# The second sweep's conv-branch channel gates moved from the merge to between the first sweep's scores

## The chip, the cores and the metric

One core of a Trainium2 chip runs the program. The metric is the device time of one execution in microseconds (us). The kernel before took 1878.28 us (median of 3 runs, 1877.82 to 1882.60).

## What is computed

One decoder layer for a prompt of 512 tokens and 64 sample tokens. A gated short convolution and a sliding-window attention run side by side; per-channel sigmoid gates merge them; a layer norm follows, and then a product-key retrieval over 128 x 128 experts (16 of 128 keys on each side, then 16 of the pairs, for each of 8 heads). Cut to what matters here:

```python
z = x @ w_in                    # b_gate, c_gate, h_in, q, k, v, g_conv, g_attn
conv_y  = short_conv(c_gate * h_in)
conv_br = (b_gate * conv_y) @ w_conv_out
attn_br = attention(q, k, v) @ w_attn_out
merged  = sigmoid(g_conv) * conv_br + sigmoid(g_attn) * attn_br
h = layer_norm(ALPHA * x + merged @ w_o)
top16 of (h @ w_pq) . sub_keys -> 16 experts a head, softmax gate
y = layer_norm(ALPHA * h + sum gate * gelu(h . expert_u[i]) * expert_v[i])
```

## The kernel before, in words

Every matmul is made of three, on values split in a high and a low part: a weight tile of 128 x 1024 is loaded on SP's queue (`raw`), rounded by ACT (`whi`, L119), and the rest is subtracted by POOL or DVE (`wlo`, L120). `table` does this, and `weight` (L580) calls it for the projections and counts the tiles of a sweep in `units`.

The tokens run in two sweeps. The first has 256 columns: prompt chunk 0, the samples and 64 more prompt rows. Its experts are fetched row by row with indirect DMAs on POOL and applied on DVE. The second has 320 columns (chunks 1 to 3) and treats its experts densely, all 128 x 128 of them, as matmuls.

Around the change the program says, in this order: the first sweep's merge, up to its normed `hT`; then the letters of `ORDER` (L62, L829): q and k project the second sweep, each s scores a quarter of the first sweep's keys (`scores`: four products with `w_pq`, matmuls with the keys, then on DVE `top16`, L413 to L417, and after every second s `route`, which gives the expert numbers), each c one of four tiles of the second sweep's convolution, each a one of its three attention chunks. Then the row work of the first sweep is made ready (`experts`, L836), and the second sweep is merged: `merge_conv` (L647) with 8 products for the conv gates (`w_g`, sigmoid on ACT at L658) and 8 with `w_cc` (multiplied on DVE at L661), and `merge_attention` (L663) with the same for the attention branch (L671 to L675), `w_o` and the norm. The tiles of attention and convolution lie in a pool `t`, which `merge_attention` closes before it opens its own, so it starts on the gates only when the last attention is done.

The row work is 384 jobs: a fetch on POOL (L511) and one DVE instruction on 128 x 1024 (L525 for the first 192, L534 for the rest). It is advanced by the generator `side`: a weight tile that is handed a pace calls `side(pace)` behind its own split. In the second sweep tiles up to `PACE_N` have pace (1, 0), but there the row work isn't made yet and nothing runs; later tiles up to 50 have (2, 1, 1) by `units % 3`, and a tile with `units % 4 == 3` is split on DVE and has no pace. `front` (the dense experts' first matmuls) has (2, 1) on its first 69 tiles, and `back` (their last matmuls, 128 steps) has 1 job a step for the first 60 and 3 a step after. What is left at the end is run without pace.

A planner puts each engine's instructions in order ahead of time: of those that its own clock takes for ready it picks the one that stands first in the program. On the chip each engine then keeps that order.

Of the kernel before, what the change touches and what calls it, by code (L numbers as in the profile page):

```python
# [17 lines left out]
AF = mybir.ActivationFunctionType  # L18
ALU = mybir.AluOpType
# [26 lines left out]
DENSE = [1, 2, 3]  # L46
# [12 lines left out]
OB = 3  # L59


ORDER = "qkscscasacsca"  # L62
FQ = 5
KEEP = 10
LAST = 2


PACE_N = 18
PACE_A, PACE_B, PACE_U, PACE_V = (1, 0), (2, 1, 1), (2, 1), (1, 3)
LO_N = 50  # L70
GATED = "aaag"
# [4 lines left out]
def step_kernel(ctx: ExitStack, tc: tile.TileContext, I: dict, O: dict):  # L76
    nc = tc.nc
    V, A, G, PE, S = nc.vector, nc.scalar, nc.gpsimd, nc.tensor, nc.sync

    pools = {}  # L80

    def pool(key, side, bufs=1):
        return tc.tile_pool(name=key, bufs=bufs, side=side)
# [18 lines left out]
    def tmp(p, shape, tag, name=None, bufs=1, dt=F32):  # L102
        return pools[p].tile(shape, dt, tag=tag, name=name or tag, bufs=bufs)
# [163 lines left out]
    def attend_prompt(c, pt, pk, ahi, alo, col):  # L267

        r = pk.shape[1]
        q0 = START[c]  # L270
        k0 = max(0, q0 - 128)
        nk = q0 + r - k0
        use = 64 if c == SMP else 0
        qT = tmp("t", [128, 4, 128], "qT", bufs=2)[:, :, :r]
        A.activation(qT, pt, AF.Copy)
        V.tensor_copy(kT_all[:, q0 + use:q0 + r], pk[:, use:])

        if c == 0:
            blocks = [(0, 128, 0, 0)]
        elif c == SMP:  # L280
            blocks = [(0, 128, 0, 0), (64, 128, 64, 1)]
        else:
            blocks = [(0, 128, 0, c), (128, r, 0, c + 1)]
        mask = mask_p[:r, k0 + 128 - q0:k0 + 128 - q0 + nk]
        o = tmp("t", [128, 4, 2, 64], "o", bufs=2)[:r]
        for kv in range(2):
            st = tmp("t", [128, 1024], "t4", bufs=3)[:r].rearrange("p (g k) -> p g k", g=4)[:, :, :nk]
            for gp2 in range(2):
                ps = bank("at")[:r]
                for j in range(2):  # L290
                    PE.matmul(ps[:, j * 256:j * 256 + nk], qT[kv * 64:kv * 64 + 64, gp2 * 2 + j, :],
                              kT_all[kv * 64:kv * 64 + 64, k0:k0 + nk], start=True, stop=True)
                V.scalar_tensor_tensor(st[:, gp2 * 2:gp2 * 2 + 2, :],
                                       ps.rearrange("p (j k) -> p j k", j=2)[:, :, :nk], SCALE,
                                       mask.unsqueeze(1).broadcast_to([r, 2, nk]), op0=ALU.mult, op1=ALU.add)
            rd = softmax_parts(st, sink_p[:r, kv * 4:kv * 4 + 4], "p")
            pT = tmp("t", [128, 1024], "t4", bufs=3).rearrange("p (b g n) -> p b g n", b=2, g=4)[:, :, :, :r]
            for b, (at, n, _, _) in enumerate(blocks):
                ps = bank("at")
                for g in range(4):  # L300
                    PE.transpose(ps[:n, g * 128:g * 128 + r], st[:, g, at:at + n], ident[:r, :r])
                src = ps[:n].rearrange("p (g n) -> p g n", g=4)[:, :, :r]
                if b == 0:
                    A.activation(pT[:n, b], src, AF.Copy)
                else:
                    V.tensor_copy(pT[:n, b], src)
            po = bank("at")[:r]
            in_order([((po[:, g * 64:(g + 1) * 64], pT[lo:n, b, g, :], v_all[lo:n, vb, kv * 64:kv * 64 + 64]),
                       dict(start=(b == 0), stop=(b == len(blocks) - 1)))
                      for g in range(4) for b, (_, n, lo, vb) in enumerate(blocks)])  # L310
            V.tensor_tensor(o[:, :, kv, :], po[:, :256].rearrange("p (g d) -> p g d", g=4),
                            rd.unsqueeze(2).broadcast_to([r, 4, 64]), op=ALU.mult)
        pa = bank("at")
        for g in range(4):
            PE.transpose(pa[:, g * 128:g * 128 + r], o[:, g].rearrange("p k d -> p (k d)"), ident[:r, :r])
        split(ahi[:, :, col + use:col + r], alo[:, :, col + use:col + r],
              pa.rearrange("p (g n) -> p g n", g=4)[:, :, use:r])

    def attend_sample(pt, pk, v, kc, vc, ahi, alo, col):
# [4 lines left out]
        qf = qT.rearrange("p b g t -> p (b g t)")  # L324
        mask_s = tmp("t", [128, 2, 192], "mask_s")
        late(mask_s, I["mask_s"])
        st = tmp("t", [128, 1024], "t4", bufs=3)[:, :768].rearrange("p (k b s) -> p k b s", k=2, b=2)
        for kv in range(2):
            r = slice(kv * 64, kv * 64 + 64)
            ps = bank("at")  # L330
            for bh in range(2):
                o0 = bh * 192
                PE.matmul(ps[:, o0 + 128:o0 + 192], qf[r, bh * 128:(bh + 1) * 128], kT[r, :], start=True, stop=True)
                for bl in range(4):
                    b = bh * 4 + bl
# [8 lines left out]
        for i in range(4):  # L344
            PE.transpose(pc[:, i * 128:(i + 1) * 128], sf[:, i, :128], ident)
            PE.transpose(pn[:64, i * 128:(i + 1) * 128], sf[:, i, 128:192], ident)
        pcn = tmp("t", [128, 2, 4, 128], "t4", bufs=3)
        pcT, pnT = pcn[:, 0], pcn[:64, 1]
        V.tensor_copy(pcT, pc.rearrange("p (i n) -> p i n", i=4))
        A.activation(pnT, pn[:64].rearrange("p (i n) -> p i n", i=4), AF.Copy)  # L350
# [210 lines left out]
    def lhs(T, k, i):  # L561
        return tuple(t[:, k, i * 128:min(i * 128 + 128, t.shape[2])] for t in T)

    def begin(w, chunks, rows, segs, smp):
        s = SimpleNamespace(w=w, chunks=chunks, n=len(chunks), rows=rows, segs=segs, smp=smp, units=0)
        s.mv = sum(rows)
        s.xs = ExitStack()
        pools["t"] = s.xs.enter_context(pool(f"t{w}", "right"))
        s.xT = pair("x", "x", 8, s.mv)
        s.pieces = iter(list(enumerate(zip(pieces[w], pieces[w][1:]))))  # L570
        load_x(s)
        return s
# [7 lines left out]
    def weight(s, src):  # L580
        s.units += 1
        if s.w == 0:
            return table(src, "w", G if s.units % 3 != 1 else V)
        if s.units > LO_N:
            return table(src, "w", G)
        pace = PACE_A if s.units <= PACE_N else PACE_B
        if s.units % 4 == 3:
            return table(src, "w", V)
        return table(src, "w", G, pace[s.units % len(pace)])

    def product(s, wt, T, ks, tag, k0=0):

        ps = bank(tag)[:, :s.mv]
        for k in range(ks):
            mm3(ps, block(wt, k0 + k), tuple(t[:, k, :s.mv] for t in T), k == 0, k == ks - 1)
        return ps
# [28 lines left out]
    def attention(s, i):  # L625
        c = s.chunks[i]
        q, k, v = s.qkv[i]

        if c in (2, 3):
            for name, t in (("ck_p", k), ("cv_p", v)):  # L630
                S.dma_start(O[name][(c - 2) * 64:(c - 1) * 64], t[(3 - c) * 64:])
        pt, pk = transpose_qk(q, k)
        if c == SMP:
            kc = tmp("g", [128, 8, 128], "g", name="kc", bufs=GBUF)
            late(kc, I["kcT"])
            vc = tmp("g", [128, 8, 128], "g", name="vc", bufs=GBUF)
            late(vc, I["vc"])
            S.dma_start(O["ck_s"][:, 120:128, :], k[:64, :])
            S.dma_start(O["cv_s"][:, 120:128, :], v[:64, :])
            attend_sample(pt, pk, v, kc, vc, *s.at, i * 128)  # L640
        attend_prompt(c, pt, pk, *s.at, i * 128)

    def conv(s, ct):
        conv_tile(ct, lambda j: product(s, weight(s, I["w_bch"][ct, j]), s.xT, 8, "u" if j else "mm"), *s.cv,
                  s.segs, s.smp)

    def merge_conv(s):  # L647

        if s.smp:
            S.dma_start(O["sc_s"], state)  # L650
        if 3 in s.chunks:
            S.dma_start(O["sc_p"], ucar)
        s.rs = ExitStack()
        pools["r"] = s.rs.enter_context(pool(f"r{s.w}", "left"))
        s.br = tmp("r", [128, 8, s.mv], "br")
        for dt in range(8):
            sg = tmp("t", [128, s.mv], ("cg", "bg")[dt % 2])
            A.activation(sg, product(s, weight(s, I["w_g"][dt, 0]), s.xT, 8, "u"), AF.Sigmoid)  # L658
            if dt % 2 == 0:
                wt = weight(s, I["w_cc"][dt // 2])  # L660
            V.tensor_tensor(s.br[:, dt, :], sg, product(s, wt, s.cv, 4, "mm", dt % 2 * 4), op=ALU.mult)  # L661

    def merge_attention(s):  # L663

# [146 lines left out]
    at_stack = ExitStack()  # L811
    pools["at"] = at_stack.enter_context(psum("at", 3))
    sel3 = ([tmp("k", [128, 128], f"k3{k}") for k in range(2)], tmp("k", [128, 128], "gt3"))
    first = begin(0, GATHER, [128, 128], [(0, 128), (192, 256)], 128)
    project_q(first)
    project_kv(first)
# [1 line left out]
        attention(first, i)  # L818
    for ct in range(4):
        conv(first, ct)  # L820
    merge_conv(first)
    merge_attention(first)
    for src, dst in (("ck", "ck_s"), ("cv", "cv_s")):
        late(O[dst][:, 0:120, :], I[src][:, 8:128, :])
    second = begin(1, DENSE, [128, 128, 64], [(0, 320)], 0)
    do = dict(q=lambda: project_q(second), k=lambda: project_kv(second), s=lambda: scores(first, count["s"]),
              c=lambda: conv(second, count["c"]), a=lambda: attention(second, count["a"]))
    count = dict.fromkeys(do, 0)
    for x in ORDER:  # L829
        do[x]()  # L830
# [218 lines left out]
```

## Time and profile before

| | us |
|---|---|
| median of 3 runs | 1878.28 |
| lowest, highest | 1877.82, 1882.60 |
| the profiled execution's own time | 1882.06 |
| its span, first to last instruction | 1880.3 |
| PE busy | 1733.5 |
| DVE busy | 1507.2 |
| POOL busy | 1111.2 |
| ACT busy | 782.1 |

PE is the matmul engine, DVE, ACT and POOL the vector, scalar and general engine; SP only issues DMAs. A row of a timeline gives the start, the duration, the engine, the line, the operation, the tiles (out<-in) and, in brackets, how long the engine had been idle and what released it. A row of a list of groups gives count, busy time, mean, and idle time before.

### The profile page before, as it was taken

Reading aid. Unit: us, or ns where it says so; the run is one execution under the profiler, and the core shown is the slowest. Engines: PE = TensorE matmul, PEld = TensorE weight load, DVE = VectorE, ACT = ScalarE, POOL = GpSimd, SP = SyncE. Lnnn points to the kernel's source line nnn. Section 1 sums busy time; section 2 is a strip of 40 time slices with the busy share of each in tenths; the row PEclk is TensorE's granted clock in tenths of the full one; section 3 lists DMA queues with packets and bytes.
Section 4 is the critical chain, followed back from the end, with each engine's and each line's share of the span. In section 5 each row is a group of like instructions: output and inputs, shape, how many; then the busy total and the mean of one; then the engine's idle time right before and its main releaser. Section 6 shows DMA issues by size and latency. Waiting matters only on the chain.

```text
span 1880.3 us, 27617 instructions
## 1 busy us (share of the span) xinstructions
PE 1733.5 (92%) x9760; PEld 1573.5 (84%) x9760; DVE 1507.2 (80%) x2632; ACT 782.1 (42%) x1339; POOL 1111.2 (59%) x724
## 2 busy tenths in 40 slices
PE   7999998897989998699979899999999999999985
PEld 7997798887779888699978777787899999998974
DVE  6646689998955699998896677878778888888897
ACT  4554343442333433367785333333333333343322
POOL 4445433466756667688835522223578777778883
PEclk9999999997989999799999899999999999999998
DMA  7445443357757678799947999999989999989973
GB/s 246 156 134 213 130 135 118 113 186 254 277 192 249 232 239 276 248 326 363 338 187 253 330 327 328 345 336 341 322 311 353 335 327 353 350 299 339 326 264 108
DMA packets 190539, 496.50 MB, mean 264 GB/s; under 512 B 17712, under 2 KB 83696, under 8 KB 187312
## 3 DMA queue, kind: packets, MB, share of 16 engines
q1 hardware_dynamic: 135104, 293.39, 45.5%
q0 software_dynamic: 55296, 201.35, 30.1%
q8 instruction: 76, 1.25, 0.3%
q14 instruction: 63, 0.52, 0.1%
HBM read 454.48 MB, written 40.54 MB: 263 GB/s over the span
## 4 chain that ended last, share of the span: by engine, by line
PE 49%; DVE 24%; DMA 10%; issue 7%; POOL 5%; ACT 5%; SPq 1%; DVEq 0%; POOLq 0%; ACTq 0%
PE acc L937 19%; PE ps L123 9%; PE ps L124 8%; PE ps L125 8%; POOL wlo L120 3%; DMA re<-spill 3%; DVE junk L525 3%; PE ps L794 2%; POOL g L511 2%; DVE wlo L120 2%; DMA raw<-in_euT 2%; ACT whi L119 1%; ACT hot L791 1%; DMA g<-in_eu,idx 1%; DVE s L415 1%
## 5 line engine op out<-in xcount | busy, mean ns | idle before, releaser
L120 POOL TENSOR_TENSOR wlo<-raw,whi 128x1024 fp32r<-128x1024 f32 x232 | 580.0, 2503 | 320.6 <-ACT whi L119 287.9
L119 ACT ACTIVATE whi<-raw 128x1024 fp32r<-128x1024 f32 x388 | 409.2, 1056 | 590.0 <-PE ps L124 235.9
L123 PE MATMUL ps<-xhi,whi 128*128 128x384 f32 (+2 forms) x1600 | 531.3, 332 | 34.3 <-ACT sp L860 27.8
L125 PE MATMUL ps<-xhi,wlo 128*128 128x384 f32 (+2 forms) x1600 | 527.4, 330 | 1.6 <-POOL wlo L120 1.6
L124 PE MATMUL ps<-xlo,whi 128*128 128x384 f32 (+2 forms) x1600 | 527.6, 330 | 0.0
L534 DVE SCALAR_TENSOR_TENSOR h<-g,pre,h 128x1024 f32<-128x1024 f32 x192 | 316.2, 1647 | 71.7 <-DMA g<-in_ev,idx 70.4
L511 POOL DMA_INDIRECT g<-in_eu,idx x192 | 206.6, 1076 | 241.3 <-DVE junk L525 186.5
L123 PEld LDWEIGHTS ps<-xhi,whi 128*128 128x128 f32 x1600 | 309.6, 194 | 44.3 <-ACT sp L860 30.3
L511 POOL DMA_INDIRECT g<-in_ev,idx x192 | 255.0, 1328 | 126.5 <-DVE h L534 87.3
L124 PEld LDWEIGHTS ps<-xlo,whi 128*128 128x128 f32 x1600 | 309.3, 193 | 3.6 <-issue 0.9
L125 PEld LDWEIGHTS ps<-xhi,wlo 128*128 128x128 f32 x1600 | 308.6, 193 | 3.0 <-POOL wlo L120 2.1
L937 PE MATMUL acc<-whi,chi 128*128 128x512 f32 x756 | 292.4, 393 | 14.7 <-ACT chi L119 8.4
L937 PE MATMUL acc<-wlo,chi 128*128 128x512 f32 x756 | 299.6, 396 | 5.7 <-POOL wlo L120 5.7
L937 PE MATMUL acc<-whi,clo 128*128 128x512 f32 x756 | 258.1, 394 | 2.1 <-DVE clo L120 2.1
L120 DVE TENSOR_TENSOR wlo<-raw,whi 128x1024 fp32r<-128x1024 f32 x156 | 204.6, 1312 | 49.1 <-ACT whi L119 48.9
L937 PEld LDWEIGHTS acc<-whi,chi 128*128 128x128 f32 x756 | 143.1, 189 | 47.1 <-ACT chi L119 11.7
L937 PEld LDWEIGHTS acc<-wlo,chi 128*128 128x128 f32 x756 | 144.1, 191 | 37.0 <-POOL wlo L120 8.2
L525 DVE SCALAR_TENSOR_TENSOR junk<-g,hp 128x1024 bf16<-128x1024 f32 x104 | 125.7, 1209 | 56.9 <-DMA g<-in_eu,idx 54.8
L937 PEld LDWEIGHTS acc<-whi,clo 128*128 128x128 f32 x756 | 143.6, 190 | 32.8 <-DVE clo L120 2.7
L785 DVE TENSOR_TENSOR hot<-pt,T 128x1024 f32<-128x1024 f32 x96 | 114.0, 1217 | 17.1 <-PE ps L794 12.1
L525 DVE SCALAR_TENSOR_TENSOR junk<-g,h 128x1024 bf16<-128x1024 f32 x88 | 123.7, 1406 | 3.1 <-DMA g<-in_eu,idx 2.8
L794 PE MATMUL ps<-hot 128*128 128x128 f32 x768 | 111.6, 289 | 15.2 <-ACT hot L791 14.0
(252 smaller groups left out, 2205.5 us busy)
## 6 DMA issues: line engine op xcount, KB each, us to landing
raw<-in_euT SPq DMA_DIRECT2D x128, 512.0 KB, 6.1
raw<-in_ev SPq DMA_DIRECT2D x128, 512.0 KB, 5.0
gd<-gb SPq DMA_DIRECT2D x24, 1024.0 KB, 5.2
gm<-gd SPq DMA_DIRECT2D x48, 512.0 KB, 9.7
raw<-in_w_g SPq DMA_DIRECT2D x32, 512.0 KB, 3.4
raw<-in_w_pq SPq DMA_DIRECT2D x32, 512.0 KB, 4.2
raw<-in_w_bch SPq DMA_DIRECT2D x24, 512.0 KB, 3.5
spill<-sp SPq DMA_DIRECT2D x60, 192.0 KB, 4.2
```

The costliest lines, as they stand in the source:

```text
L119: A.activation(hi, src, AF.Copy)
L120: return (eng or V).tensor_tensor(lo, src, hi.bitcast(F32), op=ALU.subtract)
L123: PE.matmul(ps, L[0], R[0], start=start, stop=False)
L124: PE.matmul(ps, L[0], R[1], start=False, stop=False)
L125: PE.matmul(ps, L[1], R[0], start=False, stop=stop)
L415: V.match_replace(s2, val[:, 0:8], s, -3.0e38)
L511: G.indirect_dma_start(out=rows[i], out_offset=None, in_=I[src], in_offset=bass.IndirectOffsetOnAxis(ap=idx[c][:, s:s + 1], axis=0))
L525: V.scalar_tensor_tensor(junk, g, 1.0, in_psum(c), op0=ALU.mult, op1=ALU.mult, accum_out=p)
L534: V.scalar_tensor_tensor(h_tok[c], g, p, h_tok[c], op0=ALU.mult, op1=ALU.add)
L785: V.tensor_tensor(hot, iota_ps.unsqueeze(1).unsqueeze(1).broadcast_to([128, 2, 4, 128]), T[:, 0:2, n:n + 4].unsqueeze(3).broadcast_to([128 ...
L794: newest[1] = PE.matmul(ps[:, r * 128:(r + 1) * 128], hot[:, 1, r, :], oi, start=True, stop=True).ins
L937: PE.matmul(*args, **kw)
```

## The change

`branch` opens the buffer `br` of a sweep by itself; for the second sweep that is done before the first sweep begins. `conv_gate` computes one channel gate of the conv branch straight into its slot of `br`, where two rotating tiles stood before, and `merge_conv` multiplies in place. A new letter g in `ORDER` computes two gates of the second sweep; four of them are spread over the order. `PACE_N` goes from 18 to 26, since 8 more tiles now come ahead. The tag `t4` of the attention has 2 tiles in the second sweep instead of 3.

```diff
-ORDER = "qkscscasacsca"
+ORDER = "qkgsgcsgcasgacsca"
-PACE_N = 18
+PACE_N = 26
-            st = tmp("t", [128, 1024], "t4", bufs=3)[...]
+            st = tmp("t", [128, 1024], "t4", bufs=t4[0])[...]
...
+        if of:
+            s.rs, s.br, s.gated = of.rs, of.br, 0
+        t4[0] = 3 - w
...
+    def branch(s):
+        s.rs = ExitStack()
+        pools[f"r{s.w}"] = s.rs.enter_context(pool(f"r{s.w}", "left"))
+        s.br, s.gated = tmp(f"r{s.w}", [128, 8, s.mv], "br"), 0
+
+    def conv_gate(s, dt):
+        A.activation(s.br[:, dt, :], product(s, weight(s, I["w_g"][dt, 0]), s.xT, 8, "u"), AF.Sigmoid)
+        s.gated = dt + 1
...
-        s.rs = ExitStack()
-        pools["r"] = s.rs.enter_context(pool(f"r{s.w}", "left"))
-        s.br = tmp("r", [128, 8, s.mv], "br")
         for dt in range(8):
-            sg = tmp("t", [128, s.mv], ("cg", "bg")[dt % 2])
-            A.activation(sg, product(s, weight(s, I["w_g"][dt, 0]), s.xT, 8, "u"), AF.Sigmoid)
+            if dt >= s.gated:
+                conv_gate(s, dt)
             if dt % 2 == 0:
                 wt = weight(s, I["w_cc"][dt // 2])
-            V.tensor_tensor(s.br[:, dt, :], sg, product(s, wt, s.cv, 4, "mm", dt % 2 * 4), op=ALU.mult)
+            V.tensor_tensor(s.br[:, dt, :], s.br[:, dt, :], product(s, wt, s.cv, 4, "mm", dt % 2 * 4), op=ALU.mult)
...
+    early = SimpleNamespace(w=1, mv=320)
+    branch(early)
     first = begin(0, GATHER, [128, 128], [(0, 128), (192, 256)], 128)
...
-    second = begin(1, DENSE, [128, 128, 64], [(0, 320)], 0)
+    second = begin(1, DENSE, [128, 128, 64], [(0, 320)], 0, early)
...
+              g=lambda: [conv_gate(second, second.gated) for _ in range(2)], c=lambda: conv(second, count["c"]), ...)
```

## Rows read from the trace of the kernel before

**Rows 1.** The page: busy time of the engines; PE's busy tenths in 47-us slices.
```profile
PE 1733.5 (92%) x9760; PEld 1573.5 (84%) x9760; DVE 1507.2 (80%) x2632; ACT 782.1 (42%) x1339; POOL 1111.2 (59%) x724
...
PE   7999998897989998699979899999999999999985
```
**Rows 2.** Stretches: us; busy PE, PEld, DVE, ACT, POOL (x); clock; DMA share, GB/s.
```profile
237.00:267.00 30.00, 28.85 (x200) 27.21 (x199) 22.71 (x83) 14.64 (x28) 10.37 (x5) 0.94 0.41 138
267.00:306.00 39.00, 34.57 (x245) 32.84 (x244) 38.91 (x154) 13.15 (x27) 11.83 (x5) 0.96 0.35 116
306.00:347.00 41.00, 33.34 (x227) 31.96 (x227) 41.00 (x129) 16.49 (x32) 16.38 (x7) 0.91 0.37 123
347.00:395.00 48.00, 45.67 (x302) 43.69 (x301) 48.00 (x185) 20.82 (x33) 20.20 (x8) 0.96 0.34 110
395.00:437.00 42.00, 30.80 (x192) 25.85 (x191) 39.64 (x74) 16.26 (x35) 31.57 (x19) 0.83 0.74 246
437.00:497.00 60.00, 56.49 (x312) 50.96 (x312) 54.64 (x65) 20.69 (x30) 44.99 (x26) 0.92 0.82 289
```
**Rows 3.** PE's timeline: its two longest waits of the stage, and the stage's end.
```profile
338.49 0.69 PE L301 MATMUL ps<-ident,t 128*128 128x128 f32 x2 [4.99 <-ACT t L261]
...
429.52 1.88 PE L301 MATMUL ps<-ident,t 64*128 64x64 f32 x8 [9.79 <-ACT t L261]
...
436.74 1.17 PE L123 MATMUL ps<-ahi,whi 128*128 128x320 f32 x3 [0.47 <-ACT ahi L119]
```
**Rows 4.** DVE's waits from 225 to 437 us, the longest; total, times, longest.
```profile
DVE val L413 <- ACT sc L758: 9.1, 2, 5.0
```
**Rows 5.** ACT's timeline: the first and the last conv gate of the second sweep.
```profile
363.62 0.44 ACT L658 ACTIVATE cg<-ps 128x320 f32<-128x320 f32 x1
...
411.83 0.42 ACT L658 ACTIVATE bg<-ps 128x320 f32<-128x320 f32 x1
```
**Rows 6.** PE's timeline in a 320-column product, first and last of 18 matmuls.
```profile
234.01 0.31 PE L124 MATMUL ps<-xlo,whi 128*128 128x320 f32 x1
...
236.50 0.31 PE L123 MATMUL ps<-xhi,whi 128*128 128x320 f32 x1
```
**Rows 7.** DVE groups from 275 to 437 us: row jobs.
```profile
L525 DVE SCALAR_TENSOR_TENSOR junk<-g,h 128x1024 bf16<-128x1024 f32 x10 | 15.5, 1547 | 0.0
```
**Rows 8.** ACT groups from 225 to 437 us: table loads for the gates.
```profile
L658 ACT ACT_TABLE_LOAD x3 | 3.8, 1283 | 0.1
```
**Rows 9.** The page's groups: the first 192 row jobs, by what they read.
```profile
L525 DVE SCALAR_TENSOR_TENSOR junk<-g,hp 128x1024 bf16<-128x1024 f32 x104 | 125.7, 1209 | 56.9 <-DMA g<-in_eu,idx 54.8
...
L525 DVE SCALAR_TENSOR_TENSOR junk<-g,h 128x1024 bf16<-128x1024 f32 x88 | 123.7, 1406 | 3.1 <-DMA g<-in_eu,idx 2.8
```
**Rows 10.** Stretches as in rows 2: the back steps with fronts, then without.
```profile
1320.00:1793.00 473.00, 471.82 (x2383) 428.87 (x2382) 395.21 (x343) 169.93 (x232) 362.69 (x220) 1.00 0.93 330
1793.00:1849.00 56.00, 48.37 (x203) 38.80 (x202) 49.23 (x38) 14.53 (x21) 44.40 (x27) 0.94 0.74 245
```
**Rows 11.** Groups from 1793 to 1849 us: row jobs on DVE, POOL's fetches and splits.
```profile
L534 DVE SCALAR_TENSOR_TENSOR h<-g,pre,h 128x1024 f32<-128x1024 f32 x22 | 39.9, 1816 | 6.3 <-DMA g<-in_ev,idx 5.9
...
L511 POOL DMA_INDIRECT g<-in_ev,idx x19 | 25.8, 1355 | 6.0 <-issue 2.9 <-DVE h L534 2.5 <-DVE wlo L120 0.3
L120 POOL TENSOR_TENSOR wlo<-raw,whi 128x1024 fp32r<-128x1024 f32 x8 | 19.5, 2438 | 1.8 <-ACT whi L119 1.7
```
**Rows 12.** Timelines of DVE and POOL: row jobs alone, and one beside a split.
```profile
1838.27 1.28 DVE L534 SCALAR_TENSOR_TENSOR h<-g,pre,h 128x1024 f32<-128x1024 f32 x1
...
1812.84 3.15 DVE L534 SCALAR_TENSOR_TENSOR h<-g,pre,h 128x1024 f32<-128x1024 f32 x1 [0.68 <-DMA g<-in_ev,idx]
...
1812.51 2.38 POOL L120 TENSOR_TENSOR wlo<-raw,whi 128x1024 fp32r<-128x1024 f32 x1
```
**Rows 13.** The chain that ended last, near its end: start, us, what.
```profile
1835.63 6.50 DMA g<-in_ev,idx
```
**Rows 14.** DVE's timeline: scores of chunk 1's second head pair, masked.
```profile
349.60 0.67 DVE L293 SCALAR_TENSOR_TENSOR t<-ps,mask_p 128x512 f32<-128x512 f32 x1
```

More of the change, by code (lines that the diff above doesn't have):

```diff
@@ L78, in step_kernel @@
     V, A, G, PE, S = nc.vector, nc.scalar, nc.gpsimd, nc.tensor, nc.sync
-    pools = {}
+    pools, t4 = {}, [3]
     def pool(key, side, bufs=1):
@@ L286, in attend_prompt @@
         for kv in range(2):
-            st = tmp("t", [128, 1024], "t4", bufs=3)[:r].rearrange("p (g k) -> p g k", g=4)[:, :, :nk]
+            st = tmp("t", [128, 1024], "t4", bufs=t4[0])[:r].rearrange("p (g k) -> p g k", g=4)[:, :, :nk]
             for gp2 in range(2):
@@ L296, in attend_prompt @@
             rd = softmax_parts(st, sink_p[:r, kv * 4:kv * 4 + 4], "p")
-            pT = tmp("t", [128, 1024], "t4", bufs=3).rearrange("p (b g n) -> p b g n", b=2, g=4)[:, :, :, :r]
+            pT = tmp("t", [128, 1024], "t4", bufs=t4[0]).rearrange("p (b g n) -> p b g n", b=2, g=4)[:, :, :, :r]
             for b, (at, n, _, _) in enumerate(blocks):
@@ L326, in attend_sample @@
         late(mask_s, I["mask_s"])
-        st = tmp("t", [128, 1024], "t4", bufs=3)[:, :768].rearrange("p (k b s) -> p k b s", k=2, b=2)
+        st = tmp("t", [128, 1024], "t4", bufs=t4[0])[:, :768].rearrange("p (k b s) -> p k b s", k=2, b=2)
         for kv in range(2):
@@ L346, in attend_sample @@
             PE.transpose(pn[:64, i * 128:(i + 1) * 128], sf[:, i, 128:192], ident)
-        pcn = tmp("t", [128, 2, 4, 128], "t4", bufs=3)
+        pcn = tmp("t", [128, 2, 4, 128], "t4", bufs=t4[0])
         pcT, pnT = pcn[:, 0], pcn[:64, 1]
@@ L562, in lhs, with begin @@
         return tuple(t[:, k, i * 128:min(i * 128 + 128, t.shape[2])] for t in T)
-    def begin(w, chunks, rows, segs, smp):
+    def begin(w, chunks, rows, segs, smp, of=None):
         s = SimpleNamespace(w=w, chunks=chunks, n=len(chunks), rows=rows, segs=segs, smp=smp, units=0)
         s.mv = sum(rows)
+        if of:
+            s.rs, s.br, s.gated = of.rs, of.br, 0
+        t4[0] = 3 - w
         s.xs = ExitStack()
@@ L820, in step_kernel @@
         conv(first, ct)
+    branch(first)
     merge_conv(first)
@@ L824, in step_kernel @@
         late(O[dst][:, 0:120, :], I[src][:, 8:128, :])
-    second = begin(1, DENSE, [128, 128, 64], [(0, 320)], 0)
+    second = begin(1, DENSE, [128, 128, 64], [(0, 320)], 0, early)
     do = dict(q=lambda: project_q(second), k=lambda: project_kv(second), s=lambda: scores(first, count["s"]),
-              c=lambda: conv(second, count["c"]), a=lambda: attention(second, count["a"]))
+              g=lambda: [conv_gate(second, second.gated) for _ in range(2)], c=lambda: conv(second, count["c"]), a=lambda: attention(second, count["a"]))
     count = dict.fromkeys(do, 0)
```

## The prediction, made before the change was run

> **What bounds the kernel now.** I read the page first, then the stretches around the change, then who waits for whom there, and last the end of the chain. Over the whole run PE is the fullest engine, 1733.5 of 1880.3 us, with DVE at 1507.2 [rows 1]. But the change sits in a stage that is different: from the first sweep's scores to the start of the second sweep's attention merge (237 to 437 us). There DVE is the full engine: 22.7 of 30, 38.9 of 39, 41.0 of 41, 48.0 of 48, 39.6 of 42 us, while PE has 1.2, 4.4, 7.7, 2.3 and 11.2 us to spare, 26.8 together [rows 2]. The two longest of PE's waits are for the attention's exponentials, 4.99 and 9.79 us [rows 3]. The stage ends at 436.74, when the last attention is done and `merge_attention` may take over the pool. So inside it PE's idle time costs nothing; DVE's total of work and DVE's own idle time set the end. Where does DVE idle? Its longest wait is for the scores: 9.1 us in two waits, before the first and the second s [rows 4]. The gates themselves run from 363.62 to 411.83 [rows 5], behind the last s: the planner already uses them as filler while DVE works through the routing.
>
> After that, 437 to 497 us is PE's again (56.5 of 60) [rows 2]. Far behind, from 1320 to 1793, PE is full (471.8 of 473) and three row jobs a step hide beside it; but after the last front, from 1793 to 1849, PE falls to 48.4 of 56, DVE is at 49.2 and POOL at 44.4 [rows 10], and the chain that ends last runs through the row jobs; one of its longest pieces is a fetch of 6.50 us [rows 13]. There each row job that is left counts.
>
> **The change, part by part.** Nothing is removed: the same products, splits, sigmoids and multiplications remain. Three things move.
>
> First, **8 gate products move ahead of the scores.** One is 24 matmuls at (236.50 - 234.01) / 17 = 0.146 us start to start [rows 6], 3.5 us; two a letter g, 7.0 us. One g comes before the first s, two before the second, three before the third, four (28.1 us) before the fourth. PE has 1.2 us to spare up to the second s, so that arrives up to 14.1 - 1.2 = 12.9 us later; up to the fourth it has 13.2 us [rows 2], so that arrives up to 14.9 us later. The gates give DVE almost nothing to do meanwhile: 3 of their 8 splits (tiles 7, 15, 19), the rest are POOL's and ACT's. DVE's idle time before the second s grows, by 0 if it finds attention work to draw forward, by 12.9 if not. I take 8: the first attention chunk is there to draw on, but its own steps wait on PE and ACT.
>
> Second, **8 row jobs move from the merge to the end.** `merge_conv` holds tiles 19 to 30 before and 27 to 30 after. By the pace rule the twelve tiles give 12 jobs (tiles 19, 23 and 27 have none; 21, 24 and 30 give two, the other six one), the four tiles give 4. The count closes with the trace: 12 + 20 (`merge_attention`) + 56 late ones = the 88 that read `h`, and the 69 fronts at 2 and 1 give the 104 that read `hp` [rows 9]. All paces behind stay as they are, so the jobs that are missing in front are missing until the end. In the stage, DVE did 10 jobs at 1.55 us before 437 [rows 7]; with 4 left, 6 x 1.55 = 9.3 us less, of which I take 8, since jobs of `merge_attention`'s first tiles can be drawn forward. With the first part that is 8 - 8 = 0 for the stage. Bounds: -9.3 and no later scores, and a further -5 if four POOL splits that now come in DVE's idle time no longer stretch a DVE instruction (one is stretched from 1.28 to 3.15 us beside a split [rows 12]; I count 1.3 for each), so -14; above, 14.9 without any relief, +15.
>
> Third, **the end.** Before, the paces use up the 384 jobs and one opening call in back step 122: 12 + 20 + 104 + 60 + 3 x 63 = 385. After, 8 fewer in front make the last one fall in step 125 of 128. Steps with fronts end with 118; from there on, the jobs set the pace. Eight more come there. Price of one: on DVE 1.28 us alone and 1.82 in the mean of this stretch [rows 11, 12], so 10.2 to 14.5 us; on POOL a fetch is 1.36 us [rows 11], 10.8 us; by the rate of the stretch, 56 us for 22 jobs with their splits [rows 10, 11], 20.4 us; and if they fill DVE's idle 6.8 us of that stretch first, 10.2 - 6.8 = 3.4. I take 12, between the two DVE prices, as DVE and POOL both are nearly full there. The row shows a job at 1.28 us with POOL quiet and 3.15 us beside a split of POOL [rows 12]. The Trainium skill, SBUF — State Buffer, section "Who interferes with whom", says that a DVE instruction with two SBUF inputs contends with a GpSimd one that reads SBUF; the stretched row agrees. The added jobs bring no splits with them, so by that rule they would cost the lower price, 10.2 us, 2 less than I take.
>
> The rest. The gates' loads pass the scores' and convolution's loads on SP's queue; the DMA share there is 0.34 to 0.41 [rows 2], so nothing is taken for it. POOL's splits come earlier, where POOL has 10 to 20 us busy of 30 to 48 [rows 2]: nothing. ACT changes its table more often if sigmoids fall between exponentials: a load takes 1.28 us, and the gates have already 3 in this stage [rows 8]; up to 8 more are 10 us of ACT, which is under half busy, and DVE waits little for it. I take nothing in the sum and up to 5 us for the worst case. The page ScalarE: Activation LUTs of the Trainium skill, section "What ACT_TABLE_LOAD costs", gives ~2.66 us for a switch, with a drain; by that it would be 21 us of ACT, and it speaks against sigmoids between exponentials; the 1.28 us of the load agree, the drain is in no row that I have. Two `t4` tiles instead of three make the second head pair's scores wait for the first's transposes; in the trace these come first anyway (338.49 against 349.60 [rows 3, 14]): nothing, 2 us at worst. In the first sweep the gates no longer wait for two rotating tiles, but PE is at 9 tenths there from slice 2 on [rows 1]: nothing, 1 us at best.
>
> Sum: 0 for the stage, +12 at the end. The profiled execution took 1882.06 us, so 1894; it lies 3.8 us above the median, and against the median 1878.3 + 12 = **1890 us**.
>
> **The rivals.**
> *A, faster: PE's gaps take the gates.* PE has 13.2 us to spare before the fourth s. If the gates run in its waits for DVE and not ahead of the scores, DVE is fed as before and has 9.3 us less to do and perhaps 5 less of stretching: -14 for the stage, +3.4 at the end where jobs fill idle time: 1867 us. It decides itself at the second s: if that isn't later, A holds. For it: the waits in [rows 3]. Against: they come after the second s, while two of the four letters g stand ahead of it, where PE is full.
> *B, no change: the planner moves nothing that matters.* The gates stay filler, the jobs alone move: -9.3 in the stage, +10 to 12 at the end: 1880 us. For it: the planner already runs the gates wherever PE has room [rows 5]. Against: it picks by place in the program, and they now stand ahead.
> *C, much slower: the fourth s starves DVE.* It comes 14.9 us later and the routing behind it is the last long DVE work; table loads add 5, the end 12 to 14, relief 4 to 8: +26, 1904 us. Against: DVE has a backlog by then.
>
> **How the numbers follow.** Forecast 0.46, A 0.20, B 0.18, C 0.16. About 0.3% (5.6 us) is what a measurement can tell from no change. Forecast and C are slower, B is the same, A is faster: 0.62, 0.18, 0.20. The range, 1866 to 1906, takes in A's and C's centres and the bounds between; outside lie -14 with less at the end than 3.4, and +15 with 20.4 at the end.
>
> **What would show it.** In the changed kernel's profile: the first `top16` of the second s later than 267 us by 5 to 13 (A: not later); DVE idle between 237 and 300 us longer; the attention merge's first gate within 8 us of 436.7; 88 jobs that read `h` and 104 that read `hp` as before, but 24 instead of 32 ahead of the first `hp`; the last L534 8 to 16 us later against the end of the fronts. The prediction is wrong if the attention merge starts more than 12 us earlier, or if the end, from the last front to the last instruction, grows by less than 5 us.

## The result, and the profile after

The changed kernel takes 1899.12 us (median of 6 runs, 1890.88 to 1905.80) against 1878.05 us of the kernel before beside it: ratio 1.0105, 95% interval 1.0078 to 1.0133. It is slower by about 20 us, and the forecast of 1890 us (1866 to 1906, slower 0.62) takes it in, near its upper end. Of the 20 us about 14 come from a stretch for which the sum took nothing, and the terms that it did price came near by other routes than the ones it gave.

The profiled execution took 1905.80 us, the longest of the six, so the phases below overstate the median by up to 7 us. Most lines of the kernel before stand 1 to 13 numbers further down in the kernel after. First the page: busy time of the engines, and PE's busy tenths in 40 slices. The work is that of [rows 1]; PE's slice 26 (counted from 0), among the back steps, is an 8 that was a 9.

```profile
span 1904.0 us, 27598 instructions
...
PE 1738.0 (91%) x9760; PEld 1574.4 (83%) x9760; DVE 1516.7 (80%) x2632; ACT 782.8 (41%) x1338; POOL 1102.1 (58%) x724
...
PE   7998999979799996899888899989999999999984
```

The stretches of [rows 2] in the kernel after (us; busy PE, PEld, DVE, ACT, POOL; clock; DMA share, GB/s):

```profile
237.00:267.00 30.00, 29.58 (x210) 28.14 (x208) 19.46 (x79) 15.09 (x27) 14.39 (x6) 1.00 0.46 151
267.00:306.00 39.00, 36.73 (x266) 34.82 (x265) 28.57 (x128) 18.26 (x26) 16.78 (x7) 1.00 0.48 156
306.00:347.00 41.00, 34.27 (x258) 33.14 (x256) 41.00 (x137) 20.42 (x34) 17.89 (x7) 0.98 0.37 122
347.00:395.00 48.00, 44.77 (x294) 42.23 (x295) 37.00 (x142) 19.16 (x40) 13.60 (x6) 0.91 0.28 91
395.00:437.00 42.00, 28.30 (x152) 21.54 (x152) 40.64 (x124) 11.30 (x29) 17.31 (x12) 0.68 0.47 157
```

PE is filled up to 306 us by the gates, as meant; DVE pays: it idles 10.5, 10.4 and 11.0 us in the first, second and fourth stretch, where [rows 2] has 7.3, 0.1 and 0. DVE's timeline shows the start of the second s (before: 267.09):

```profile
281.29 0.87 DVE L414 MAX8 val<-sc 128x8 f32<-128x128 f32 x4 [6.21 <-ACT sc L768]
```

DVE's waits from 225 to 437 us, after and then before, show that the longer idle time isn't spent at the scores: those waits are 9.8 us where [rows 4] has 9.1. New are 14.1 us for weight tiles that ACT hasn't rounded yet (`whi`), when DVE stands at their low halves.

```profile
DVE wlo L121 <- ACT whi L120: 14.1, 5, 4.9
DVE val L414 <- ACT sc L768: 9.8, 2, 6.2
```

```profile
DVE wlo L120 <- ACT whi L119: 1.3, 2, 0.7
```

The gates on ACT now run from 221.51 to 329.37 (ACT's timeline; [rows 5] has 363.62 to 411.83). PE's timeline at the end of the stage has the product behind the last attention at 435.07 (436.74 in [rows 3]): the stage ends where it did.

```profile
221.51 0.44 ACT L657 ACTIVATE br<-ps 128x320 f32<-128x320 f32 x1
...
329.37 0.44 ACT L657 ACTIVATE br<-ps 128x320 f32<-128x320 f32 x1
```

```profile
435.07 1.17 PE L124 MATMUL ps<-ahi,whi 128*128 128x320 f32 x3 [0.47 <-ACT ahi L120]
```

**Where the time went.** ACT rounds the coefficients of the back steps into two tiles `chi` in turn, so those of step 6 must wait until PE has done step 4. ACT's timeline dates the steps by this: "steps 4 to 60" is the time from the rounding of step 6 to that of step 62. The coefficients of the first 60 steps come back from `spill`, so this stretch is called the spilled steps below. Its two ends in after (before: 1085.30 and 1330.49):

```profile
1080.13 0.53 ACT L120 ACTIVATE chi<-re 128x384 fp32r<-128x384 f32 x1 [2.60 <-PE acc L950]
...
1341.79 0.51 ACT L120 ACTIVATE chi<-gel 128x384 fp32r<-128x384 f32 x1
```

The same has been read from every profile; with the end of the second sweep's norm (DVE's last `xlo`) this gives the phases below, in us, worked out from the timelines. Lines other than the first are differences to before; the last column is the ratio of the runs' times to those of the kernel before on the same chip.

```
                          end of  norm to  steps   steps   steps    116 to  span    ratio of times
                          norm    step 4   4-60    60-100  100-116  end             [95%]
before                    530.1   555.2    245.2   332.3   134.3    83.2    1880.3
after                     -2.7    -2.5     +16.5   -2.3    +4.8     +9.9    +23.7   1.0105 [1.0078, 1.0133]
e1 jobs only              -0.3    -0.7     +9.2    -1.1    +6.5     +8.9    +22.4   1.0090 [1.0063, 1.0117]
e2 gates only             +8.6    -1.9     +9.1    -1.9    -1.4     -1.1    +11.4   1.0071 [1.0045, 1.0097]
e3 buffers only           -1.1    -1.8     -2.6     0.0    -1.4      0.0     -6.9   1.0001 [0.9977, 1.0025]
e4 jobs in fronts         -7.2    -4.0     +10.5   -1.7    -0.3     -0.5     -3.2   1.0018 [0.9991, 1.0046]
e6 after, SP of before    -1.4    -4.6     +8.6    -1.1    +5.2     +9.0    +15.7   1.0087 [1.0060, 1.0115]
e7 before, SP of after    +1.5    -3.7     +5.7    -0.6    +4.0     +2.1     +9.0   1.0030 [1.0015, 1.0045]
e8 before + 8 jobs, SP    +3.0    -4.9     +13.2   +1.0    +1.0     -5.0     +8.3   1.0043 [1.0021, 1.0064]
e9 before, alternating    +0.4    +2.9     -0.3     0.0    -0.3     +1.9     +4.6   1.0013 [0.9992, 1.0033]
e10 after, plan of before -3.2    -1.5     -0.7     0.0    -1.0     +9.2     +2.8   1.0031 [1.0015, 1.0048]
e11 before, plan of after +1.7    -0.5     +9.1    -2.4    +1.4     +1.1    +10.5   1.0082 [1.0051, 1.0112]
e12 e4, plan of before    -0.3    -2.3     -1.0     0.0    -0.1     +1.2     -2.5   0.9956 [0.9936, 0.9976]
e13 before + 8, its plan  -0.4    -3.3     -2.6     0.0    +0.4     -2.7     -8.7   0.9964 [0.9944, 0.9983]
```

A row is one execution, and the times of one kernel spread over 5 to 20 us, so a difference of 2 or 3 us in one cell says little; the pattern down a column, and the ratios, carry the weight.

### The profile page after: what moved, and what is told of

It reads as the page before. It is cut to its first block, busy times and chain, and to the rows that moved or that the text cites. A ratio compares the mean times of both kernels' runs of the same rounds, so it can differ in the third digit from the quotient of the medians.

```text
span 1904.0 us, 27598 instructions
## 1 busy us (share of the span) xinstructions
PE 1738.0 (91%) x9760; PEld 1574.4 (83%) x9760; DVE 1516.7 (80%) x2632; ACT 782.8 (41%) x1338; POOL 1102.1 (58%) x724
## 4 chain that ended last, share of the span: by engine, by line
DVE 26%; PE 25%; DMA 22%; issue 12%; POOL 8%; ACT 4%; SPq 1%; POOLq 0%; DVEq 0%; ACTq 0%
DMA g<-in_ev,idx 12%; PE acc L950 8%; POOL g L512 4%; POOL wlo L121 4%; PE ps L124 4%; PE ps L126 4%; PE ps L125 4%; DVE junk L526 3%; PE ps L804 3%; DVE wlo L121 3%; DMA raw<-in_ev 2%; DMA re<-spill 2%; DVE h L535 2%; ACT whi L120 2%; ACT hot L801 1%
## 5 line engine op out<-in xcount | busy, mean ns | idle before, releaser
L512 POOL DMA_INDIRECT g<-in_eu,idx x192 | 200.8, 1046 | 276.5 <-DVE junk L526 224.6
L535 DVE SCALAR_TENSOR_TENSOR h<-g,pre,h 128x1024 f32<-128x1024 f32 x192 | 308.1, 1605 | 58.1 <-DMA g<-in_ev,idx 56.0
L950 PE MATMUL acc<-whi,clo 128*128 128x512 f32 x756 | 263.0, 397 | 2.8 <-DVE clo L121 2.8
L950 PEld LDWEIGHTS acc<-whi,chi 128*128 128x128 f32 x756 | 145.2, 192 | 55.0 <-ACT chi L120 18.9
```

Of the source, the lines that this page charges most:

```text
L512: G.indirect_dma_start(out=rows[i], out_offset=None, in_=I[src], in_offset=bass.IndirectOffsetOnAxis(ap=idx[c][:, s:s + 1], axis=0))
L535: V.scalar_tensor_tensor(h_tok[c], g, p, h_tok[c], op0=ALU.mult, op1=ALU.add)
L950: PE.matmul(*args, **kw)
```

## Experiments: which half of the change costs what

The change does two things that can be parted: gates early, and 8 row jobs fewer in the stage.

**Jobs only.** The kernel before, with the 8 tiles 19 to 26 handing out no row job.

```diff
-        return table(src, "w", G, pace[s.units % len(pace)])
+        return table(src, "w", G, 0 if 18 < s.units <= 26 else pace[s.units % len(pace)])
```

> The kernel before, with tiles 19 to 26 of the second sweep handing out no row jobs: 4 jobs run in the conv merge instead of 12, the gates stay where they were, all buffers as before. Theory 1 (the 8 late jobs cost the time, and not only at the end: they also shift where the first 128 jobs run out, which the trace of the changed kernel shows at the start of the back steps): the attention merge starts 6 to 10 us earlier, the first 60 back steps take some 10 us longer than before (270 against 257 us), the end grows by 10, total +8 to +18 us. Theory 2 (the early gates or the buffers bring the loss in the back steps): the back steps take as long as before, total 0 to +4 us.

Measured 1897.93 us, 1.0090 of before. The end grows by 8.9 us, as in after, with nothing else moved: this is what 8 late jobs cost here. In front they give no relief (the attention merge, expected 6 to 10 us earlier, starts at 439.42 instead of 436.74, and the norm ends 0.3 us earlier): there the jobs had been hidden.

**Gates only.** The kernel after, with its three pace tiles 28 to 30 handing out 4 jobs each, so that all 12 are drawn there.

```diff
-        return table(src, "w", G, pace[s.units % len(pace)])
+        return table(src, "w", G, 4 if 27 < s.units <= 30 else pace[s.units % len(pace)])
```

> The changed kernel with the row jobs given back: the conv merge's three tiles with a pace hand out 4 jobs each, 12 in all as before; the gates stay early. Theory 1: the attention merge starts 5 to 10 us later than in the kernel before (scores later, no relief), back steps and end as in the kernel before, total +3 to +10 us. Theory 2: the first 60 back steps lose 14 us as in the changed kernel, total +15 to +25 us.

Measured 1894.84 us, 1.0071, some 13 us, between what the two theories said. The end is that of before (-1.1), and the norm ends 8.6 us later. PE's waits from 437 to 545 us, of this kernel and then of before, show how:

```profile
PE ps L730 <- DVE h L201: 17.0, 3, 10.8
```

```profile
PE ps L720 <- DVE h L200: 9.9, 3, 5.2
```

PE stands behind DVE's norm for 7.1 us more. With the scores late the expert numbers `idx` are late (the first come at 420.8 us, in before at 394.7), so where 10 jobs ran ahead of 437 us in before, 5 do now, and the rest crowd in front of the norm. In after, with 8 of them gone, this wait is 10.7 us.

**Buffers only.** The kernel after with the old order and pace limit, so that only `br` and the two `t4` tiles remain of the change.

```diff
-ORDER = "qkgsgcsgcasgacsca"
+ORDER = "qkscscasacsca"
-PACE_N = 26
+PACE_N = 18
```

> The changed kernel with the order and the pace bound of the kernel before: the early buffer, gates written straight into it and two attention tiles remain, but all gates run in the conv merge, with 12 jobs. Theory 1: within 3 us of the kernel before. Theory 2 in its form with the buffers: the first 60 back steps lose 14 us, total +12 to +16 us.

Measured 1879.02 us, 1.0001: the buffers cost nothing, as predicted.

**Jobs in the fronts.** The kernel after, with the 8 missing jobs handed out in the first 8 fronts.

```diff
-PACE_U[t % len(PACE_U)] if t < AHEAD else 0
+PACE_U[t % len(PACE_U)] + (t < 8) if t < AHEAD else 0
```

> The changed kernel, with each of the first 8 fronts handing out one row job more, in a stretch where DVE is busy for 54 of 108 us. So the 8 jobs are made up for before the back steps, and the gates stay early. Theory 1: back steps and end as in the kernel before, the stage before them 5 us shorter, as in the changed kernel: -5 us, some 1873 us. Theory 2: the back steps lose 14 us as in the changed kernel, and only the end comes back: +8 to +12 us.

Measured 1885.60 us, 1.0018. The end is back (-0.5), the norm is 7.2 us early, and still no time is won: the steps 4 to 60 lose 10.5 us. The second theory has the steps right, but not its total of 8 to 12 us.

That loss stands in after, e1, e2 and e4, whatever the jobs and gates do, and not in e3. The steps hold the same loads and products; only their speed differs. Stretches of the steps 4 to 60, before and then after (columns as in [rows 2]):

```profile
1085.30:1330.50 245.20, 236.79 (x1033) 193.85 (x1032) 192.96 (x285) 85.82 (x115) 62.77 (x57) 0.99 0.98 336
```

```profile
1080.10:1341.80 261.70, 243.97 (x1046) 199.85 (x1045) 193.07 (x293) 87.20 (x116) 58.41 (x57) 0.97 0.93 317
```

The DMAs are the full resource there, 0.98 of the time at 336 GB/s before, and 0.93 at 317 after. DVE's work is the same to 0.1 us. PE idles 17.7 us instead of 8.4 and is busy 7.2 us longer, at a granted clock of 0.97 of the full one instead of 0.99 and with 1046 matmuls in the stretch instead of 1033.

## Experiments: why the spilled steps are slower

What does differ is the order in which the planner queued these steps, 600 us behind the edit. All kernels whose earlier work had shifted (after, e1, e2, e4) share another order than before and e3, and their profiles show the engines keeping it. On SP's queue, with v an `ev` table, r a `re` tile and G a third of `gm`, the last 16 of these steps stand as:

```
before  GGG vrvrvrvrvrvrvrvr GGG vrvrvrvrvrvrvrvr
after   GGG vrvrrvvvrrrvvr   GGG vrrvrvvrvrvrvrvrvr
```

The first theory was that this order of transfers alone is the cause. Four kernels tested it. Each links SP's transfers of these steps by edges that fix the order of issue and wait for nothing.

```diff
+SPQ = "vrvrvrvrvrvGGGvrvrvrvrvvrrrvvGGG...vrvrvrvrvrvrvrvrGGG"
...
+    def queue_order(line):
+        at, last = dict(v=6, r=5, G=6), None
+        for k in SPQ:
+            ins = line[k][at[k]]
+            at[k] += 1
+            if last is not None:
+                tc.add_manual_dep(ins, last.name, ..., reason="queue")
+            last = ins
```

After with the order of before:

> The kernel after, with one thing forced: the order in which SP's queue holds the transfers of the spilled back steps (the expert rows of ev, the spilled re tiles, the gm tiles) is that of the kernel before, instruction for instruction; the engines' work is that of the kernel after. The page of after has the back steps 4 to 60 in 261.7 us, before in 245.2. Theory (the order itself costs the time: runs of three ev loads and three re loads in a row instead of an alternation): steps 4 to 60 in 243 to 249 us, the time 12 to 18 us below after, 1881 to 1888. Rival (the order is only a companion; the steps are slower because of what the early gates left behind in front of them, or by the spread of one execution): 256 to 264 us, the time within 5 us of after, 1895 to 1903.

Before with the order of after:

> The kernel before, with one thing forced: SP's queue holds the transfers of the spilled back steps in the order of the kernel after. Nothing of the gates is moved. Theory (the order itself): steps 4 to 60 in 254 to 262 us against 245.2, the time 8 to 16 us above before, 1886 to 1895. Rival (only a companion): 243 to 248 us and the time within 4 us of before, 1875 to 1883.

Before with 8 jobs more in the fronts (the edit of e4) and its own order held:

> The kernel before with one more row job handed out in each of the first 8 fronts (so 8 jobs fewer are left for the end), and SP's order of the spilled back steps held at that of the kernel before. Theory of the end (the 8 jobs of the last steps cost 1.2 us each there and less in the fronts, as after and the kernel with fewer jobs in the stage lost 9 to 10 us there): the stretch after back step 116 takes 73 to 79 us against 83.2, the fronts no more than 3 us longer, the time 4 to 10 us below before, 1868 to 1875. Rival (before already has all the jobs that the end can hide, the ones taken away had cost nothing): the end stays at 82 to 84 us and the time is that of before or up to 5 us above it, since the fronts carry the jobs: 1877 to 1884.

Before with a plain alternation all through:

> The kernel before with SP's order of the spilled back steps made a plain alternation (one ev load, one re load, and three gm loads every eight steps) all through; before has that in its second half only. Theory (runs of equal transfers in the queue cost the time): steps 4 to 60 in 236 to 243 us against 245.2, the time 2 to 8 us below before, 1870 to 1877. Rival (what is lost depends on something else than the clusters): 244 to 248 us, the time within 3 us of before.

Measured 1895.26 (1.0087), 1887.13 (1.0030), 1889.80 (1.0043) and 1884.74 us (1.0013). The theory falls in this form. With SP's order restored, after still needs 253.8 us for the steps 4 to 60, half of the loss; before with the other order needs 250.9 there, 5.7 more than its own 245.2 and less than the 254 to 262 of the theory, and its ratio says 5.6 us, below the 8 to 16 asked for (the -3.6 us that the expectation of e11 below gives for this is a misreading: its stretch began two roundings late); a plain alternation gains nothing; and e8, in SP's order of before, loses 13.2 us in these steps, which eats the 5.0 us that its end gains.

Nor do these four hold everything else still. Their timelines show that with SP's order forced the planner gave DVE and ACT new orders too: in e6 and e8 the same one, which is neither that of before nor that of after, and in e7 yet another. Only e9 left both nearly as in before. So e6 to e8 don't tell what SP's queue alone is worth.

In e6, however, the rest of the loss sat in the steps 4 to 20 (77.8 us against 70.2) and 52 to 56 (22.3 against 19.8), the steps between had before's pace again, and DVE's queue was still irregular in places. So the second theory took in the three queues that the planner had reordered together: SP's transfers, DVE's products with gm (m), lo halves of coefficients and tables (c, w) and row jobs (J), and ACT's hi halves. From the built programs, DVE's order in the same place:

```
before  w J c m w J c m w J c m w J c m w J c m
after   w J w J m m w J c c m c w J m w J c m m w J c c
```

The next four kernels hold all three, step for step, by the same kind of edges:

```diff
+DVEQ = ('m5 c4 w6 J133 c5 m6 w7 J134 c6 w8 J135 ... J183 c54 m55 w57')
+ACTQ = ('W4 C3 W5 C4 W6 C5 W7 C6 W8 W9 C7 W10 ... C54 W57')
...
+        for q, plan in zip(queues[1:], (DVEQ, ACTQ)):
+            q += [line[x[0]][int(x[1:])] for x in plan.split()]
```

After with the plan of before in the spilled steps:

> The kernel after, in which the spilled back steps are queued as in the kernel before on SP (ev, re and gm loads), on DVE (products with gm, the lo halves of both splits, the row jobs) and on ACT (the hi halves), step for step; with SP's order alone held, steps 4 to 60 took 253.8 us against 261.7 of after and 245.2 of before. The gates, the stage before and the number of row jobs are those of after. Theory (the order of the three queues together is what the spilled steps lose to; holding SP's alone left DVE's and ACT's irregular groups): steps 4 to 60 in 243 to 248 us, the time 9 to 16 us below after, 1885 to 1891 where before is 1880. Rival (the orders are companions; the steps are slower because each row job in them is an eu row 8 jobs later, or from what is left of the stage): 252 to 262 us, 1893 to 1901.

Before with the plan of after:

> The kernel before, in which the spilled back steps are queued as in the kernel after on SP, DVE and ACT; nothing else is changed. Theory (the three orders together cost the time): steps 4 to 60 in 253 to 262 us against 245.2, the time 8 to 17 us above before, 1888 to 1897 where before is 1880. Rival (companions; SP's order alone had moved these steps by -3.6 us): 241 to 248 us, the time within 6 us of before, 1876 to 1886.

After with 8 jobs in the fronts and the plan of before:

> The kernel after with one more row job in each of the first 8 fronts (1885.6 us, steps 4 to 60 in 255.7) and the spilled back steps queued as in the kernel before on SP, DVE and ACT. Theory of the orders: steps 4 to 60 in 243 to 248, the time 6 to 12 us below that kernel's ratio of 1.0018, that is 0.9955 to 0.9985 of before, 1871 to 1877: early gates and 8 jobs moved out of the stage into the fronts then beat both kernels. Rival (companions): 252 to 258 us and a ratio of 1.000 to 1.004.

Before with 8 jobs in the fronts and its own plan:

> The kernel before with one more row job in each of the first 8 fronts, and the spilled back steps queued as in before on SP, DVE and ACT (with SP's alone held: steps 4 to 60 in 258.4 us, the end 5 us shorter than before's, ratio 1.0043). Theory of the orders: steps 4 to 60 in 243 to 249, the end still 4 to 6 us shorter, the ratio 0.994 to 0.999, 1869 to 1878. Rival (it is the 8 jobs themselves that the steps feel: which row comes in which step): 253 to 260 us, ratio 1.003 to 1.006.

Measured 1886.12 us (1.0031), 1894.80 (1.0082), 1874.03 (0.9956) and 1873.58 (0.9964). The theory holds both ways. The profiles' timelines fall into two groups. In before, e3, e10, e12 and e13 these steps stand in one order on all three queues and need 242.6 to 245.2 us; in after, e1, e2, e4 and e11 they stand in the other (in e11 nearly) and need 254.3 to 261.7, whatever the gates and the number of jobs. The plan of before takes after from 1.0105 to 1.0031, the plan of after takes before from 1 to 1.0082: 14 and 15 us, and the steps 4 to 60 follow, as the stretches of e10 and then e11 show:

```profile
1080.70:1325.20 244.50, 235.48 (x1034) 192.73 (x1033) 192.68 (x293) 85.50 (x115) 59.27 (x57) 1.00 0.98 339
```

```profile
1086.50:1340.80 254.30, 241.52 (x1047) 198.53 (x1046) 193.13 (x285) 87.31 (x115) 62.84 (x57) 0.98 0.95 326
```

What the order does is seen in the waits of this stretch (total, times, longest). First before, then after:

```profile
PE acc L937 <- ACT chi L119: 8.4, 8, 1.8
...
ACT whi L119 <- DMA raw<-in_ev: 34.0, 11, 6.6
...
DVE clo L120 <- PE acc L937: 2.6, 5, 1.1
```

```profile
PE acc L950 <- ACT chi L120: 16.4, 6, 4.2
...
ACT whi L120 <- DMA raw<-in_ev: 49.5, 12, 7.3
...
DVE clo L121 <- PE acc L950: 11.8, 11, 3.6
```

In e10 the three are back at 8.7, 37.4 and 2.2 us, in e11 they are 12.8, 43.4 and 8.6. A reading of these waits, which no run tests by itself: where the order puts several table halves ahead of a coefficient, ACT stands at a table whose transfer hasn't landed while PE waits for the coefficient behind it, and DVE waits for PE in turn. One place in after, ACT's timeline and then DVE's:

```profile
1207.77 1.06 ACT L120 ACTIVATE whi<-raw 128x1024 fp32r<-128x1024 f32 x1 [7.26 <-DMA raw<-in_ev]
1209.83 0.52 ACT L120 ACTIVATE chi<-re 128x384 fp32r<-128x384 f32 x1 [1.00 <-DVE re L920]
```

```profile
1209.19 0.56 DVE L920 TENSOR_TENSOR re<-re,gm 128x384 f32<-128x384 f32 x1 [6.28 <-DMA re<-spill]
```

Both stand still for over 6 us. While they do, the transfers under way land at full rate, but no buffer comes free for the next one, and just behind it the DMAs, the full resource, run dry. Stretches of after around this place:

```profile
1201.00:1210.00 9.00, 6.58 (x30) 5.10 (x28) 2.73 (x5) 1.23 (x2) 1.14 (x2) 1.00 1.04 377
1210.00:1213.00 3.00, 2.59 (x11) 2.18 (x12) 3.00 (x6) 1.42 (x2) 0.70 (x1) 1.00 0.55 195
```

Which of the three queues matters most wasn't separated further: forcing SP's order, with what the planner then did to the other two, took back about half of the steps' loss in one direction (e6) and brought 5.7 us of e11's 9.1 in the other (e7).

e12 and e13 beat both kernels, by 0.4%, and they are level with each other: once the order is held and 8 more jobs run in the fronts, the early gates gain nothing. With the plan held, these 8 jobs take 12 to 14 us off the early gates (e10 to e12) and 7 off before (e13). In e12 the end is 8.0 us shorter than in e10, and the steps 4 to 60 are the same (244.2 and 244.5 us); what else it gains isn't in its profile, which is that of the slowest of its 12 executions. In e13, where before's end is relieved, the end gives only 2.7 us, less than the 4 to 6 expected. One profile of each doesn't settle how the rest divides.

## Why the prediction was right, point by point

The measured time lies in the range, and the kernel is slower, as forecast. Much of that is luck: two thirds of the loss came from a stretch that no term and no rival had, and the priced terms came out near for reasons other than those given.

**Scores later, +8.** Near in size, but by another route and at another place. The second s came 14.2 us later (267.09 to 281.29), just past the 12.9 that PE's spare time allowed and the 5 to 13 named. Rival A, which needed it not later, fell with that. The 8 us don't show in the stage: it ends at 435.07 against 436.74 in after, and e2, with all jobs kept, ends it no later either (433.59). What shows is 8.6 us at the norm's end in e2, 100 us on, from jobs that crowd there and not from DVE idling before the second s. So the reading that DVE's total sets the end of the stage was wrong: in after DVE is busy 23.6 us less of these 200 us (166.7 against 190.3), and the last attention still ends at the same time. What sets that end instead is open.

**Fewer jobs, -8.** Near in size with the gates early, but at the norm and not in the stage: from e2 to after the norm's end moves by 11.3 us (538.7 to 527.4), from e2 to e4 by 15.9. In before it would have been 0 (e1: -0.3). The two terms together gave 0 for the stage; measured -1.7 at its end and -2.7 at the norm's. Row jobs in the stage, DVE's groups from 275 to 437 us ([rows 7] has 10 at 1547 ns):

```profile
L526 DVE SCALAR_TENSOR_TENSOR junk<-g,h 128x1024 bf16<-128x1024 f32 x5 | 6.1, 1218 | 0.2 <-DMA g<-in_eu,idx 0.2
```

**The count.** 88 jobs still read `h` and 104 `hp`, as in [rows 9]; 23 of the 88 stand ahead of the first `hp`, 31 in before: 8 fewer, as predicted, whose 24 and 32 count the opening call in. The page's groups of after:

```profile
L526 DVE SCALAR_TENSOR_TENSOR junk<-g,hp 128x1024 bf16<-128x1024 f32 x104 | 125.9, 1211 | 58.9 <-DMA g<-in_eu,idx 56.7
...
L526 DVE SCALAR_TENSOR_TENSOR junk<-g,h 128x1024 bf16<-128x1024 f32 x88 | 119.9, 1362 | 2.3 <-DMA g<-in_eu,idx 2.2
```

**The end, +12.** Measured +9.9 in after, +8.9 in e1, +9.0 in e6, +9.2 in e10, and about 0 in every kernel that has as many jobs left for it as before (-1.1 to 2.1): that 8 late jobs cost some 9 us here is shown. The price of one was wrong all the same. The working priced a late job at its instruction on DVE, 1.28 to 1.82 us [rows 11, 12]. In fact the last job comes 18.7 us later behind the last front (38.5 us behind it in before, 57.2 in after), more than the 8 to 16 named. That is 2.3 us a job, near the rate of the stretch (56 / 22 = 2.5) that the working had only as its upper price. About half of it doesn't count, because before had slack that the sum left out: there the last job is done 15 us ahead of PE's last product, in after it is done 3 us behind it, and PE's last product stands where it stood, 53.4 and 53.7 us behind the last front. DVE's last job and PE's last product, in before and then in after (the last front's `gel` ends at 1810.3 and at 1825.2):

```profile
1847.49 1.29 DVE L534 SCALAR_TENSOR_TENSOR h<-g,pre,h 128x1024 f32<-128x1024 f32 x1
...
1863.31 0.40 PE L134 MATMUL acc<-whi,sp 128*128 128x512 f32 x1
```

```profile
1881.06 1.28 DVE L535 SCALAR_TENSOR_TENSOR h<-g,pre,h 128x1024 f32<-128x1024 f32 x1
...
1878.49 0.40 PE L135 MATMUL acc<-whi,sp 128*128 128x512 f32 x1
```

All the profiles agree: in the kernels with 8 late jobs more than before the last one is done 56.6 to 57.6 us behind the last front, with as many as before 37.0 to 39.1, with 8 fewer (e8, e13) 18.5 to 18.9, and PE's last product is 50.2 to 55.4 us behind it in all of them. It fits that 8 jobs fewer than before gain less than 8 more cost (5.0 and 2.7 us in e8 and e13). A price too low by half and a slack that was left out made the +12 come near. The groups of DVE from step 116 to the end, after and then before:

```profile
L535 DVE SCALAR_TENSOR_TENSOR h<-g,pre,h 128x1024 f32<-128x1024 f32 x28 | 42.3, 1509 | 10.0 <-DMA g<-in_ev,idx 9.7
```

```profile
L534 DVE SCALAR_TENSOR_TENSOR h<-g,pre,h 128x1024 f32<-128x1024 f32 x20 | 35.4, 1768 | 6.2 <-DMA g<-in_ev,idx 5.9
```

The mean of a job falls from 1768 to 1509 ns: the last 8 in after come behind POOL's last split, at 1.28 to 1.30 us each. That agrees with the Trainium skill, SBUF — State Buffer, section "Who interferes with whom", by whose rule on two SBUF inputs the prediction's working expected the undisturbed price. That the 10.2 us worked out from it lie near the measured 8.9 to 9.9 says nothing for the rule, though: these 8 instructions begin 2.5 us apart (1863.6 to 1881.1), so their own length isn't what a late job costs.

**The terms at nothing.** Buffers: nothing (e3). Table loads: the gates cause 4 in this stage where [rows 8] has 3, 1.28 us more of ACT.

```profile
L657 ACT ACT_TABLE_LOAD x4 | 5.1, 1283 | 0.1
```

The Trainium skill, ScalarE: Activation LUTs, section "What ACT_TABLE_LOAD costs", adds a drain of about 1.38 us to each switch. The trace of before doesn't show it: between a sigmoid and an exponential of the first sweep stand 1.28 us of load and 0.04 us more.

```profile
80.74 0.38 ACT L658 ACTIVATE cg<-ps 128x256 f32<-128x256 f32 x1
81.14 1.28 ACT L261 ACT_TABLE_LOAD   x1
82.44 0.45 ACT L261 ACTIVATE t<-t,sngm 128x192 f32<-128x192 f32 x1
```

**What failed.** The step "all paces stay as they are" was taken to mean that nothing between the stage and the end would change. Paces and work did stay; the order of the queues in the spilled steps did not, and that cost 14 us of the 20 (1.0105 against 1.0031 with the plan of before). The remaining 6 us are the priced terms as they came out: the end's 9 less some 3 to 5 in front. So the forecast of +12 lies between the change's own +6, and +20 with the planner's answer to it. The sign stands without that answer: with the plan of before the change is still slower (1.0031 [1.0015, 1.0048]). The size is near only because the range is wide and the errors partly cancel: the end priced 2 to 3 us high, the relief in front taken too small, the spilled steps left out. Between the steps 100 and 116 after, e1 and e6 lose a further 4.8 to 6.5 us and e7, which has no late jobs, 4.0; the other kernels lose 1.4 or less, and how this comes about is open. Rival C's 1904 us lies nearer to the measured 1899 than the forecast, but not for its reason: the routing did start late, and the stage ended on time all the same.

## What to carry to other kernels

Where a planner fixes the queues' orders, an edit can change the order of a stage far behind it that it doesn't touch; in a stage where the DMAs are full, compare the order of its queues before and after, and hold it if it matters, before the edit itself is judged. Work that is moved to a stretch near the end costs what its whole chain takes there, fetch and issue included (here 2.3 us for an instruction of 1.28 us), less the slack that the stretch still had; look for both before pricing it. Work that had been hidden gives nothing back when it leaves.

## What the runs showed of the hardware

The same transfers of the same sizes ran at 336 to 339 GB/s (before, e10) or at 317 to 326 (after, e11), depending on the order in which three queues held their work. PE's granted clock over the stretch was lower where PE had more gaps, 0.97 and 0.98 of the full clock (after, e11) against 0.99 and 1.00 (before, e10): after idles 9.3 us more there than before and is busy 7.2 us more, with 1% more matmuls.

A row job on DVE took 1.28 us alone and 3.15 us beside a split of POOL [rows 12]. A change of ACT's table took 1.28 us of load and no drain that a row shows.
